# Samples' arrays of the second layer moved once per eight groups, and DeltaNet's diagonal blocks of 16 moved through scratch in 7 transfers a head

## The chip, the core and the metric

The kernel runs on one core of one Trainium2 chip, as one program of 54048 instructions. The metric is the device time of that core in microseconds (us). The engines are named as the profile names them: PE is the matrix engine (PEld its weight loads), DVE the vector engine, ACT the scalar engine, POOL the GpSimd engine, and SP the engine whose one queue issues every transfer of this kernel. SP issues them in the order in which they stand, and one that waits holds all that stand behind it.

## What is computed

One inference step of a two-layer recurrent model over a prompt of 2048 tokens and over 8 samples of one token each; all arithmetic is in 32-bit floats. Layer 0 runs an RG-LRU and a gated DeltaNet beside each other, layer 1 an S5 state space model:

```python
def trunk(x, c, ...):                      # once for the prompt, once for the samples
    for i in range(DEPTH):                 # DEPTH = 2
        h = rms_norm(x, w["norm_w"][i]) * (1.0 + scale) + shift
        if i % 2 == 0: y, ... = ab_mixer(h, ...)
        else:          y, sr, si = s5_mixer(h, ...)
        x = x + gate * y
    return rms_norm(x, w["final_norm_w"]), states

# gated DeltaNet, per head: chunks of 64 tokens
A = where(strict, einsum(k_beta, k) * decay, 0)
sol = triangular_solve(A + eye, rhs, lower=True)      # needs the inverse of A + I
S, o = scan over the chunks

# S5, per group of 16 channels (64 groups) and 64 complex states
Bu = einsum(B_bar, u);  Bu[0] += A_bar * x0
xs = associative_scan(A_bar, Bu)
y  = einsum(C, xs).real + d * u;  y = gelu(y);  ...
```

For the samples S5 is one step: state = A_bar * x0 + B_bar u, and the output is C state + d u.

## The kernel before

**Layer 0** runs in two halves of 1024 tokens (the first with the 8 samples beside it, so its arrays have 1032 columns), eight heads each. Each head is a row of products of the normed input with 128 columns of weights (the units k, xa, q, v, za, gw and zb). `in_unit` makes one of them: every product is three matmuls (high part by high part, high by low, low by high), PE's line L876, into groups of PSUM banks that ACT or DVE copies out. Halves with samples use groups of 384, 384 and 264 columns (`BLS`), the others two of 512 (`BL0`); four banks ("ps_mm") serve them.

**Background work.** Everything else is written as Python generators in a list (`Fibers`). `bg.pump` takes one step of each lane whenever 1536 columns of products have been written, so that DeltaNet, the RG-LRU, the S5 tables and S5 itself stand between the products in program order. A scheduler then orders each engine's instructions by its own estimate of times; instructions made through `VH` and `AH` (line L127) get a higher priority there. So a changed set of instructions can change the order of others, and engines wait for each other at run time wherever the estimate was off.

**DeltaNet's inverse** (`gdn_prep`, once per head, 16 times). It needs inverses of the 16x16 diagonal blocks of 8 chunks (64 blocks). A tile `AT` (128 partitions, 8 chunks, 128 columns) holds A transposed; its diagonal blocks go to DRAM scratch `fsd` in 8 transfers (L966) and come back as `fsA` with one block on each of 64 partitions (L970). Fifteen steps on DVE (`fsP` L1004, `fsT` L1006) make the inverses, `fsT`, and `fsU`, their transposes. Both are stored to scratch `fst` (L1010, L1011), and 16 small transfers read them back into three tiles: `zt` (even blocks), `zo` (odd blocks) and `U32` (block pairs of 32, zeroed by a GpSimd memset before, L1015). `gdn_main` of the same head uses them as weights on PE: `zt` at L1053, `zo` at L1065, `U32` after it.

**S5** (`s5`, lines L1702 to L1796) runs in two halves too, 8 blocks of 8 groups each; a block has two quads of 4 groups. Block i is added to lane i mod 2, so two blocks overlap. A quad loads three tables (`s5RT`, `s5ct`, `s5st`), PE projects (L1729), DVE rotates, scans and rotates back (`s5t`, ending with the sum X = X + ... that the text calls "the last sum"), a table `s5O` is loaded, and PE makes the output (L1786 with the table `MT`, L1787 with X and `s5O`).

In the first half a quad also carries the samples: it loads the old states `s5xa` and, with halves swapped, `s5xb` (one and two transfers), and their inputs `s5uo`. PE makes B u (L1740), ACT copies it, PE transposes it (L1749). DVE makes a·s5xa, b·s5xb, adds them, and adds what PE transposed; then PE multiplies by C (`cs8`, two transfers a block, L1776), DVE adds d·u, ACT applies gelu. New states and outputs (`dYs`) are stored for each quad. That makes 14 transfers a block for the samples. The second half (no samples) is the same code without them.

`s5_tables` (once per block, in the background of layer 0) loads a tile `gp` with five transfers, four of them for C.

Of the kernel before, what the change touches and what calls it, by code (L numbers as in the profile page):

```python
# [9 lines left out]
I32 = mybir.dt.int32  # L10
AF = mybir.ActivationFunctionType
OP = mybir.AluOpType
# [58 lines left out]
def hybrid_step(ctx: ExitStack, tc: tile.TileContext, I, O, dump=None):  # L71
# [14 lines left out]
    def K(name, shape, dt=FT):  # L86
        return kp.tile(list(shape), dt, name=name, tag=name)
# [23 lines left out]
    def D(name, shape, dt=FT):  # L111
        return dr.tile(list(shape), dt, name=name, tag=name)

    def dma(out, in_):
        SP.dma_start(out, in_)  # L115
# [33 lines left out]
    def bc(ap, shape):  # L149
        return ap.to_broadcast(list(shape))  # L150
# [30 lines left out]
    def wait(n):  # L181
        for _ in range(n):
            yield
# [291 lines left out]
    a1 = K("a1", (128, 2, 64))  # L475
# [151 lines left out]
    def s5_tables(mt):  # L627
# [5 lines left out]
        for off, x, y in ((624, "cre", "cim"), (752, "cim", "cre")):  # L633
            dma(gp[0:64, off:off + 128].rearrange("p (g c) -> p g c", c=16), I[x][:, g8])
            dma(gp[64:128, off:off + 128].rearrange("p (g c) -> p g c", c=16), I[y][:, g8])
# [96 lines left out]
    fsd = [D(f"fsd{i}", (8, 128, 16)) for i in range(2)]  # L732
    fst = [D(f"fst{i}", (2, 64, 256)) for i in range(2)]
    ss0 = {1: K("ss0", (128, 8))}
# [177 lines left out]
    def gdn_prep(hf, h, g, ready):  # L912
# [54 lines left out]
        for b in range(8):  # L967
            dma(fd[:, 16 * b:16 * b + 16, :].rearrange("u j i -> j u i"),
                AT[16 * b:16 * b + 16, :, 16 * b:16 * b + 16])
        F = TT("fsA", (64, 16, 16))  # L970
        dma(F.rearrange("p j i -> p (j i)"),
            fd.rearrange("u (b j) i -> (u b) (j i)", b=8))
# [40 lines left out]
        zt, zo = TT("zt", (128, 8, 16)), TT("zo", (128, 8, 16))  # L1013
        U32 = g["U32"] = TT("U32", (128, 8, 32))
        G.memset(U32, 0.0)  # L1015
        fb = [ft[n].rearrange("(u b) (i j) -> b i u j", b=8, i=16) for n in range(2)]
        for b in range(4):
            r = 32 * b
            dma(zt[r:r + 16], fb[0][2 * b])
            dma(zo[r:r + 16], fb[1][2 * b + 1])  # L1020
            dma(U32[r:r + 16, :, 0:16], fb[1][2 * b])
            dma(U32[r + 16:r + 32, :, 16:32], fb[1][2 * b + 1])
# [679 lines left out]
    def s5(hf, mt, uc, yg, upad):  # L1702
        Q3 = (128, 4, 128)
        yield from wait(9)
# [3 lines left out]
        if hf == 0:  # L1708
            cs8 = TT("cs8", (128, 8, 16))
            dma(cs8[0:64], I["cre"][:, mt * 8:mt * 8 + 8])  # L1710
            dma(cs8[64:128], I["cim"][:, mt * 8:mt * 8 + 8])
            VH.tensor_scalar(cs8, cs8, nsg[:, 0:1], None, op0=OP.mult)
        for qd in range(2):
# [5 lines left out]
            if hf == 0:  # L1719
                xa_, xb_ = TT("s5xa", (128, 4, 8)), TT("s5xb", (128, 4, 8))  # L1720
                dma(xa_, I["s5x"][:, g4, :])
                dma(xb_[0:64], I["s5x"][64:128, g4, :])
                dma(xb_[64:128], I["s5x"][0:64, g4, :])
                uo = TT("s5uo", (16, 4, 8))
                dma(uo, dUs[mt].rearrange("(c g) b -> c g b", g=8)[:, qd * 4:qd * 4 + 4, :])
# [10 lines left out]
            if hf == 0:  # L1736

                ps = PS("ch", (128, 128))
                for j in range(4):
                    PE.matmul(ps[32 * j:32 * j + 32], upad[:, qd * 32:qd * 32 + 32], tl["RT"][:, j, :],  # L1740
                              start=True, stop=True)
                us = TT("s5us", (128, 128))
                AH.activation(us, ps, AF.Copy)
                VH.tensor_tensor(xa_, xa_, bc(a1[:, 0, g4, None], (128, 4, 8)), op=OP.mult)
                VH.tensor_tensor(xb_, xb_, bc(a1is[:, g4, None], (128, 4, 8)), op=OP.mult)
                VH.tensor_tensor(xa_, xa_, xb_, op=OP.add)
                yield from wait(2)
                pws = PS("ch", (128, 4, 40))
                PE.transpose(pws.rearrange("p j c -> p (j c)")[:, 0:128], us, ident)  # L1749
                VH.tensor_tensor(xa_, xa_, pws[:, :, 0:8], op=OP.add)  # L1750
                dma(O["s_s5"][:, g4, :], xa_)
# [21 lines left out]
            if hf == 0:  # L1773
                pys = PS("ch", (128, 4, 8))
                for j in range(4):
                    PE.matmul(pys[0:16, j, :], cs8[:, qd * 4 + j, :], xa_[:, j, :],  # L1776
                              start=True, stop=True)
                VH.tensor_tensor(uo, uo, bc(d16[:, g4, None], (16, 4, 8)), op=OP.mult)
                VH.tensor_tensor(uo, uo, pys[0:16], op=OP.add)
                AH.activation(uo, uo, AF.Gelu_apprx_tanh)  # L1780
                dma(dYs[mt][:, qd * 32:qd * 32 + 32], uo.rearrange("c g b -> c (g b)"))
# [188 lines left out]
def layouts(x_prompt, x_sample, c_prompt, c_sample, state_conv_a, state_lru, state_conv_b,  # L1970
# [6 lines left out]
    def cols(v, n):  # L1977
# [30 lines left out]
        "s5x": np.concatenate([state_s5_re[0], state_s5_im[0]], axis=2).transpose(2, 1, 0),  # L2008
        "w1": c_in_w[0].reshape(8, 128, 16, 8, 16).transpose(2, 1, 0, 4, 3).reshape(16, 128, 1024),
# [8 lines left out]
        "cre": s5_c_re[0].transpose(2, 0, 1),  # L2018
        "cim": s5_c_im[0].transpose(2, 0, 1),
# [52 lines left out]
```

## Time and profile before

| | |
|---|---|
| median of 3 runs | 3163.17 us (3158.49 to 3163.83) |
| the profiled execution | 3162.53 us, its span 3160.6 us |
| busy: PE, DVE, ACT, POOL | 2946.8, 2077.0, 1109.6, 689.1 us |
| mean granted clock of PE | 0.967 of full speed |

The profile is of one execution. Its span runs from the first instruction to the last; some 2 us of the execution lie around it. Layer 0 takes most of it up to about 2130 us; S5's first half lies at about 2210 to 2525 us and its second at about 2700 to 2960 us, with products of layer 1 between and after. "Idle before" of an instruction is the time for which its engine had nothing to do right before it, and the name behind the arrow is what ended that.

### The profile page before, as it was taken

What the parts mean: (1) busy time and instruction counts of PE and PEld (TensorE: products, weight loads), DVE (VectorE), ACT (ScalarE), POOL (GpSimd) and SP (SyncE); (2) the same over time, 40 slices, a digit from 0 to 9 for tenths busy, and PEclk for the clock granted to TensorE, in tenths of its full rate; (3) what the DMA queues carried; (4) which work ended last, traced back from release to release, by engine and by line L of the source; (5) the groups of instructions that cost most, each with busy time, mean ns of one, the idle gap of its engine ahead of it and who ended that gap; (6) DMA issues with size and microseconds to landing.
All of it is one profiled execution on the core that took longest, in us unless ns stands there. A gap on an engine that the chain in (4) does not pass through costs nothing.

```text
span 3160.6 us, 54048 instructions
## 1 busy us (share of the span) xinstructions
PE 2946.8 (93%) x19958; PEld 2577.6 (82%) x19958; DVE 2077.0 (66%) x5468; ACT 1109.6 (35%) x2023; POOL 689.1 (22%) x672
## 2 busy tenths in 40 slices
PE   5999998999999999999999999999978899989998
PEld 3888888888887777777777777899868899877786
DVE  7896986677894877866756787445655534565524
ACT  3544444444543324433334343412211233110222
POOL 3233433223442323021111111101112222000100
PEclk8999999999999999999999999999989899999999
DMA  6344344443537873444434324555566548587442
GB/s 231 123 134 155 116 160 152 134 143 133 168 125 262 274 227 125 130 128 157 122 129 144 122 88 138 180 182 200 185 218 214 184 144 293 196 298 248 150 134 87
DMA packets 404136, 532.09 MB, mean 168 GB/s; under 512 B 143520, under 2 KB 210592, under 8 KB 403872
## 3 DMA queue, kind: packets, MB, share of 16 engines
q1 hardware_dynamic: 403872, 528.63, 51.0%
q8 instruction: 158, 2.59, 0.3%
q14 instruction: 106, 0.87, 0.1%
HBM read 328.11 MB, written 200.36 MB: 167 GB/s over the span
## 4 chain that ended last, share of the span: by engine, by line
PE 57%; DVE 26%; DMA 7%; issue 4%; ACT 2%; POOL 2%; SPq 2%; DVEq 0%; POOLq 0%; ACTq 0%
PE ps_mm L876 44%; DVE s5t L127 4%; DVE c_v L856 2%; SPq L115 2%; DVE xc L856 1%; DVE fsP L1004 1%; DMA yk<-yd 1%; DVE c_q L856 1%; DVE fsT L1006 1%; PE ps_pre L1787 1%; POOL wlo L234 1%; DVE D L910 1%; PE ps_ch L1139 1%; PE ps_ch L1145 1%; PE ps_pre L1786 1%
## 5 line engine op out<-in xcount | busy, mean ns | idle before, releaser
L876 PE MATMUL ps_mm<-hh,wlo 128*128 128x512 f32 (+2 forms) x2536 | 791.6, 373 | 0.0
L876 PE MATMUL ps_mm<-hh,whi 128*128 128x512 f32 (+2 forms) x2536 | 761.5, 361 | 4.7 <-DVE sz L1872 2.3
L876 PE MATMUL ps_mm<-hl,whi 128*128 128x512 f32 (+2 forms) x2536 | 748.7, 356 | 0.0
L876 PEld LDWEIGHTS ps_mm<-hl,whi 128*128 128x128 f32 x2536 | 480.2, 192 | 44.5 <-issue 0.2
L876 PEld LDWEIGHTS ps_mm<-hh,whi 128*128 128x128 f32 x2536 | 472.3, 192 | 53.5 <-DVE sz L1872 2.7
L876 PEld LDWEIGHTS ps_mm<-hh,wlo 128*128 128x128 f32 x2536 | 449.9, 192 | 35.7 <-issue 7.7
L234 POOL TENSOR_TENSOR wlo<-wraw,whi 128x512 fp32r<-128x512 f32 (+1 forms) x200 | 277.3, 1394 | 664.9 <-ACT whi L233 429.5
L876 PE MATMUL ps_mm<-yl,whi 128*128 128x512 f32 (+2 forms) x640 | 187.9, 356 | 3.0 <-DVE yl L234 3.0
L876 PE MATMUL ps_mm<-yh,whi 128*128 128x512 f32 (+2 forms) x640 | 185.1, 358 | 5.8 <-ACT yh L233 5.8
L876 PE MATMUL ps_mm<-yh,wlo 128*128 128x512 f32 (+2 forms) x640 | 189.8, 359 | 0.0
L233 ACT ACTIVATE whi<-wraw 128x512 fp32r<-128x512 f32 (+1 forms) x200 | 121.9, 618 | 119.5 <-DMA wraw<-in_wo 42.5
L1136 ACT ACTIVATE qs<-ps_ch,geg 128x128 f32<-128x128 f32 x128 | 47.1, 368 | 297.7 <-DVE rr L1133 293.8
L856 DVE SCALAR_TENSOR_TENSOR c_k<-raw,cbw,c_k 128x256 f32<-128x256 f32 x192 | 91.0, 513 | 73.7 <-ACT c_k L893 72.8
L876 PEld LDWEIGHTS ps_mm<-yh,whi 128*128 128x128 f32 x640 | 118.3, 191 | 17.9 <-ACT yh L233 7.3
L876 PEld LDWEIGHTS ps_mm<-yl,whi 128*128 128x128 f32 x640 | 119.9, 191 | 15.6 <-DVE yl L234 4.8
L876 PEld LDWEIGHTS ps_mm<-yh,wlo 128*128 128x128 f32 x640 | 118.3, 191 | 9.8
L892 ACT ACTIVATE raw<-ps_mm 128x384 f32<-128x384 f32 (+1 forms) x160 | 81.6, 513 | 74.4 <-PE ps_mm L876 70.9
L876 PE MATMUL ps_mm<-y2h,whi 128*128 128x384 f32 (+3 forms) x344 | 100.4, 340 | 0.1
L876 PE MATMUL ps_mm<-y2h,wlo 128*128 128x384 f32 (+3 forms) x344 | 99.9, 339 | 0.0
L876 PE MATMUL ps_mm<-y2l,whi 128*128 128x384 f32 (+3 forms) x344 | 99.6, 338 | 0.0
L856 DVE SCALAR_TENSOR_TENSOR c_v<-raw,cbw,c_v 128x256 f32<-128x256 f32 x192 | 95.1, 529 | 4.0 <-ACT c_v L893 3.8
L856 DVE SCALAR_TENSOR_TENSOR xc<-raw,caw,xc 128x256 f32<-128x256 f32 x192 | 94.7, 514 | 4.2 <-ACT xc L893 3.5
(669 smaller groups left out, 5754.2 us busy)
## 6 DMA issues: line engine op xcount, KB each, us to landing
wraw<-in_w SPq DMA_DIRECT2D x128, 256.0 KB, 3.8
whw<-whi SPq DMA_DIRECT2D x128, 256.0 KB, 2.5
wlw<-wlo SPq DMA_DIRECT2D x128, 256.0 KB, 2.4
whi<-whw SPq DMA_DIRECT2D x128, 256.0 KB, 4.4
wlo<-wlw SPq DMA_DIRECT2D x128, 256.0 KB, 4.2
modw<-in_modw SPq DMA_DIRECT2D x48, 512.0 KB, 5.7
yk<-yd SPq DMA_DIRECT2D x32, 512.0 KB, 5.8
xk<-x1d SPq DMA_DIRECT2D x32, 512.0 KB, 5.7
```

What stands on the lines that cost most here:

```text
L115: SP.dma_start(out, in_)
L127: return getattr(self.eng, op)(*args, **kw)
L233: a = A.activation(hi, src, AF.Identity)
L234: return a, (lo_eng or V).tensor_tensor(lo, src, f(hi), op=OP.subtract)
L856: V.scalar_tensor_tensor(d, raw[:, a * n + j:a * n + j + n], wt[:, tile_i, j:j + 1], d, op0=OP.mult, op1=OP.add)
L876: PE.matmul(p, w[:, c], x[:, b0:b1], start=(k == 0 and x is hh[k] and w is wh), stop=(k == 7 and w is wl))
L892: A.activation(raw[:, 3 + b0:3 + e], p[:, 0:e - b0], AF.Copy)
L910: V.tensor_scalar(dc[:, c], dc[:, c], tok["gc"][:, c, h:h + 1], 0.0, op0=OP.subtract, op1=OP.min)
L1004: V.tensor_tensor(pr_[:, 0:i, 0:i], Ti[:, 0:i, 0:i].rearrange("p j c -> p c j"), bc(F[:, 0:i, i].unsqueeze(1), s), op=OP.mult)
L1006: V.tensor_reduce(Ti[:, i, 0:i], pr_[:, 0:i, 0:i], axis=AX.X, op=OP.add, negate=True)
L1136: A.activation(qs, p1[:, 1, :], AF.Copy, scale=g["eg"][:, c:c + 1])
L1139: PE.matmul(p2_, U[:, c, :], rr, start=True, stop=True)
```

## The change

DeltaNet: `AT` is stored whole, in one transfer, to scratch whose rows are spaced so that the 16x16 blocks on the diagonal lie at one fixed stride, and `fsA` is read from there. `fst` is read back by three transfers over 128 (or 112) partitions: `zu` (all transposed blocks), `zt` and `zo`. The tile U32 is no longer zeroed and loaded; ACT makes its two halves from `zu` by a copy with a scale that is 0 or 1 on each partition (`odd`, made once at the start). S5: the inputs come in layouts that let `cs8`, `s5xa`, `s5xb`, `s5uo` be loaded by one transfer each per block; the three products with them on DVE are done once per block behind the load of `cs8`, and the new states and outputs are stored once per block. `s5_tables` takes two transfers for C where it took four.

```diff
         C8 = (128, 8, 16)
-        for off, x, y in ((624, "cre", "cim"), (752, "cim", "cre")):
-            dma(gp[0:64, off:off + 128].rearrange("p (g c) -> p g c", c=16), I[x][:, g8])
-            dma(gp[64:128, off:off + 128].rearrange("p (g c) -> p g c", c=16), I[y][:, g8])
+        for off, x in ((624, "cri"), (752, "cir")):
+            dma(gp[:, off:off + 128].rearrange("p (g c) -> p g c", c=16), I[x][:, g8])
         zero = TB("zero")
...
     gcd = [D(f"gcd{i}", (8, 8, 128)) for i in range(2)]
-    fsd = [D(f"fsd{i}", (8, 128, 16)) for i in range(2)]
+    fsd = [D(f"fsd{i}", (8, 128 * 129)) for i in range(2)]
     fst = [D(f"fst{i}", (2, 64, 256)) for i in range(2)]
...
+    oi, odd = TT("oddi", (128, 1), I32), K("odd", (128, 2))
+    G.iota(oi, pattern=[[0, 1]], base=0, channel_multiplier=1)
+    V.tensor_scalar(oi, oi, 4, 1, op0=OP.logical_shift_right, op1=OP.bitwise_and)
+    V.tensor_copy(odd[:, 1:2], oi)
+    V.tensor_scalar(odd[:, 0:1], odd[:, 1:2], -1.0, 1.0, op0=OP.mult, op1=OP.add)
     ss0 = {1: K("ss0", (128, 8))}
...
         fd, ft = fsd[par], fst[par]
-        for b in range(8):
-            dma(fd[:, 16 * b:16 * b + 16, :].rearrange("u j i -> j u i"),
-                AT[16 * b:16 * b + 16, :, 16 * b:16 * b + 16])
...
+        dma(fd[:, 0:128 * 128].rearrange("u (p i) -> p u i", i=128), AT)
         F = TT("fsA", (64, 16, 16))
-        dma(F.rearrange("p j i -> p (j i)"),
-            fd.rearrange("u (b j) i -> (u b) (j i)", b=8))
+        dma(F, fd.rearrange("u x -> (u x)").rearrange("(q x) -> q x", x=16 * 129)[:, 0:16 * 128]
+            .rearrange("q (j i) -> q j i", i=128)[:, :, 0:16])
         Ti = TT("fsT", (64, 16, 16))
...
         dma(ft[1], Tu.rearrange("p i j -> p (i j)"))
-        zt, zo = TT("zt", (128, 8, 16)), TT("zo", (128, 8, 16))
+        zt, zo, zu = (TT(n, (128, 8, 16)) for n in ("zt", "zo", "zu"))
         U32 = g["U32"] = TT("U32", (128, 8, 32))
-        G.memset(U32, 0.0)
-        fb = [ft[n].rearrange("(u b) (i j) -> b i u j", b=8, i=16) for n in range(2)]
-        for b in range(4):
-            r = 32 * b
-            dma(zt[r:r + 16], fb[0][2 * b])
-            dma(zo[r:r + 16], fb[1][2 * b + 1])
-            dma(U32[r:r + 16, :, 0:16], fb[1][2 * b])
-            dma(U32[r + 16:r + 32, :, 16:32], fb[1][2 * b + 1])
+        fb = [ft[n].rearrange("(u b) (i j) -> (b i) u j", b=8, i=16) for n in range(2)]
+        dma(zu, fb[1])
+        dma(zt, fb[0])
+        dma(zo[0:112], fb[1][16:128])
+        for t in range(2):
+            A.activation(U32[:, :, 16 * t:16 * t + 16], zu, AF.Copy, scale=odd[:, t:t + 1])
         while "v" not in ready:
...
         Q3 = (128, 4, 128)
+        g8 = slice(mt * 8, mt * 8 + 8)
+        if hf == 0:
+            G8 = (128, 8, 8)
+            xa_, xb_, uo = TT("s5xa", G8), TT("s5xb", G8), TT("s5uo", (16, 8, 8))
+            dma(xa_, I["s5x"][:, g8])
+            dma(xb_, I["s5xs"][:, g8])
+            dma(uo, dUs[mt].rearrange("(c g) b -> c g b", g=8))
         yield from wait(9)
...
             cs8 = TT("cs8", (128, 8, 16))
-            dma(cs8[0:64], I["cre"][:, mt * 8:mt * 8 + 8])
-            dma(cs8[64:128], I["cim"][:, mt * 8:mt * 8 + 8])
+            dma(cs8, I["cri"][:, g8])
             VH.tensor_scalar(cs8, cs8, nsg[:, 0:1], None, op0=OP.mult)
+            VH.tensor_tensor(xa_, xa_, bc(a1[:, 0, g8, None], G8), op=OP.mult)
+            VH.tensor_tensor(xb_, xb_, bc(a1is[:, g8, None], G8), op=OP.mult)
+            VH.tensor_tensor(xa_, xa_, xb_, op=OP.add)
+            VH.tensor_tensor(uo, uo, bc(d16[:, g8, None], (16, 8, 8)), op=OP.mult)
         for qd in range(2):
...
                 dma(tl[n].rearrange("p g n -> p (g n)"), src[mt][:, cs])
-            if hf == 0:
-                xa_, xb_ = TT("s5xa", (128, 4, 8)), TT("s5xb", (128, 4, 8))
-                dma(xa_, I["s5x"][:, g4, :])
-                dma(xb_[0:64], I["s5x"][64:128, g4, :])
-                dma(xb_[64:128], I["s5x"][0:64, g4, :])
-                uo = TT("s5uo", (16, 4, 8))
-                dma(uo, dUs[mt].rearrange("(c g) b -> c g b", g=8)[:, qd * 4:qd * 4 + 4, :])
+            l4 = slice(qd * 4, qd * 4 + 4)
             yield from wait(6)
...
                 AH.activation(us, ps, AF.Copy)
-                VH.tensor_tensor(xa_, xa_, bc(a1[:, 0, g4, None], (128, 4, 8)), op=OP.mult)
-                VH.tensor_tensor(xb_, xb_, bc(a1is[:, g4, None], (128, 4, 8)), op=OP.mult)
-                VH.tensor_tensor(xa_, xa_, xb_, op=OP.add)
                 yield from wait(2)
...
                 PE.transpose(pws.rearrange("p j c -> p (j c)")[:, 0:128], us, ident)
-                VH.tensor_tensor(xa_, xa_, pws[:, :, 0:8], op=OP.add)
-                dma(O["s_s5"][:, g4, :], xa_)
+                VH.tensor_tensor(xa_[:, l4], xa_[:, l4], pws[:, :, 0:8], op=OP.add)
+                if qd == 1:
+                    dma(O["s_s5"][:, g8, :], xa_)
             yield from wait(2)
...
                 for j in range(4):
-                    PE.matmul(pys[0:16, j, :], cs8[:, qd * 4 + j, :], xa_[:, j, :],
+                    PE.matmul(pys[0:16, j, :], cs8[:, qd * 4 + j, :], xa_[:, qd * 4 + j, :],
                               start=True, stop=True)
-                VH.tensor_tensor(uo, uo, bc(d16[:, g4, None], (16, 4, 8)), op=OP.mult)
-                VH.tensor_tensor(uo, uo, pys[0:16], op=OP.add)
-                AH.activation(uo, uo, AF.Gelu_apprx_tanh)
-                dma(dYs[mt][:, qd * 32:qd * 32 + 32], uo.rearrange("c g b -> c (g b)"))
+                VH.tensor_tensor(uo[:, l4], uo[:, l4], pys[0:16], op=OP.add)
+                if qd == 1:
+                    AH.activation(uo, uo, AF.Gelu_apprx_tanh)
+                    dma(dYs[mt], uo.rearrange("c g b -> c (g b)"))
             yield from wait(8)
...
         "s5x": np.concatenate([state_s5_re[0], state_s5_im[0]], axis=2).transpose(2, 1, 0),
+        "s5xs": np.concatenate([state_s5_im[0], state_s5_re[0]], axis=2).transpose(2, 1, 0),
         "w1": c_in_w[0].reshape(8, 128, 16, 8, 16).transpose(2, 1, 0, 4, 3).reshape(16, 128, 1024),
...
         "bim": s5_b_im[0].transpose(1, 0, 2),
-        "cre": s5_c_re[0].transpose(2, 0, 1),
-        "cim": s5_c_im[0].transpose(2, 0, 1),
+        "cri": np.concatenate([s5_c_re[0], s5_c_im[0]], axis=2).transpose(2, 0, 1),
+        "cir": np.concatenate([s5_c_im[0], s5_c_re[0]], axis=2).transpose(2, 0, 1),
         "s5d": s5_d[0].reshape(8, 8, 16),
```

Three places in the order of instructions are used below.

ACT, first head of the first half, after the RG-LRU's square root (`tt`) and ahead of the copies that free the PSUM groups of unit zb (`zbs`). Before:

```order
L1195 ACT_TABLE_LOAD
L1195 ACTIVATE tt_1402<-tt_1402 128x1032
L521 ACT_TABLE_LOAD
L521 ACTIVATE unit1_1648<-s5ab_1645 128x64
L1640 ACT_TABLE_LOAD
L1640 ACTIVATE zbs_1448<-ps_mm_1469 128x384
L1640 ACTIVATE zbs_1448<-ps_mm_1470 128x384
```

The same place with the change:

```order
L1197 ACT_TABLE_LOAD
L1197 ACTIVATE tt_1401<-tt_1401 128x1032
L1024 ACTIVATE U32_1555<-zu_1554,odd_174 128x8x16 x2
L1642 ACT_TABLE_LOAD
L1642 ACTIVATE zbs_1447<-ps_mm_1468 128x384
L1642 ACTIVATE zbs_1447<-ps_mm_1469 128x384
```

The two copies into U32 stand ahead of `zbs`, and they wait for the transfer that fills `zu`. In about 12 of the 16 heads they stand so, in the others near the copy of unit za.

SP, same head, from the stores of the inverses on. Before:

```order
L115 DMA fst_171<-fsT 64x256
L115 DMA fst_171<-fsU 64x256
L115 DMA whw_1_1_2027<-whi 128x512
L115 DMA wlw_1_1_2028<-wlo 128x512
L115 DMA zt<-fst_171 16x8x16
L115 DMA zo<-fst_171 16x8x16
L115 DMA U_1555<-fst_171 16x8x16 x2
L115 DMA zt<-fst_171 16x8x16
L115 DMA zo<-fst_171 16x8x16
```

With the change:

```order
L115 DMA fst_171<-fsT 64x256
L115 DMA fst_171<-fsU 64x256
L115 DMA whw_1_1_2015<-whi 128x512
L115 DMA wlw_1_1_2016<-wlo 128x512
L115 DMA zu<-fst_171 128x8x16
L115 DMA zt<-fst_171 128x8x16
L115 DMA zo<-fst_171 112x8x16
L115 DMA zd_165<-zbs 128x1024
L115 DMA yd<-gx 128x1024
```

Sixteen reads have become three, `zu` first; the weights' transfers around them kept their places.

PE, S5's first half, where the sample product of one quad (`s5xa` by `cs`) and the output of the quad before it (`MT`, then `s5O`) follow each other. Before, at the block whose C is cs8_26505:

```order
L876 MATMUL ps_mm<-hh,whi 128x384
L876 MATMUL ps_mm<-hl,whi 128x384
L876 MATMUL ps_mm<-hh,wlo 128x384
L1786 MATMUL ps_pre<-uc,MT 128x128 x2
L1776 MATMUL ps_ch<-s5xa,cs_26505 16x8 x4
L1787 MATMUL ps_pre<-s5t_26529,s5O_26635 128x128
L1786 MATMUL ps_pre<-uc,MT 128x128
```

The same block with the change (its C is cs8_26512); eleven rows of products of unit kind L881 (L876 before) follow the sample product, then the first one with `s5O`:

```order
L881 MATMUL ps_mm<-hh,whi 128x384 x2
L881 MATMUL ps_mm<-hl,whi 128x384 x2
L881 MATMUL ps_mm<-hh,wlo 128x384 x2
L1780 MATMUL ps_ch<-s5xa,cs_26512 16x8 x4
L1790 MATMUL ps_pre<-uc,MT 128x128
L881 MATMUL ps_mm<-hh,whi 128x264
L881 MATMUL ps_mm<-hl,whi 128x264
L881 MATMUL ps_mm<-hh,wlo 128x264
L881 MATMUL ps_mm<-hh,whi 128x264
```

From the third block on, the sample product of one quad stands directly ahead of the output of the quad before it at four places in the order before and at two with the change; at the others layer products stand between them.

DVE, S5's first half, around the addition of PE's transposed part to `s5xa` (row `s5xa<-s5xa,ps_ch`). Before, for the first quad of one block (its states are s5xa_26515), while the last sum of the quad ahead of it (s5t1_26529) is made:

```order
L127 TENSOR_TENSOR s5t1_26529<-s5st_26470,s5t2_26530 64x4x127 x2
L127 TENSOR_TENSOR s5xb_26516<-s5xb_26516,l1_25126 128x32
L127 SCALAR_TENSOR_TENSOR s5t2_26588<-rho8_145,l1_25126,s5t1_26587 128x128
L127 TENSOR_TENSOR s5t1_26529<-s5t1_26529,s5ct_26469 128x512
L127 TENSOR_TENSOR s5xa_26515<-s5xa_26515,s5xb_26516 128x32
L127 SCALAR_TENSOR_TENSOR s5t2_26588<-rho8_145,l1_25126,s5t1_26587 128x128
L127 TENSOR_TENSOR s5xa_26515<-s5xa_26515,ps_ch_26665 128x32
L127 SCALAR_TENSOR_TENSOR s5t2_26588<-rho8_145,l1_25126,s5t1_26587 128x128 x2
```

With the change, at the corresponding place (states s5xa_26441, quad ahead s5t1_26504):

```order
L127 TENSOR_TENSOR s5t1_26504<-s5st_26471,s5t2_26505 64x4x127 x2
L127 TENSOR_TENSOR s5t1_26595<-ps_pre_26590,s5ct_26520 128x512
L127 TENSOR_TENSOR s5t1_26504<-s5t1_26504,s5ct_26470 128x512
L127 TENSOR_TENSOR s5t2_26596<-ps_pre_26590,s5st_26521 64x512 x2
L127 TENSOR_TENSOR s5xa_26441<-s5xa_26441,ps_ch_26651 128x32
L127 TENSOR_TENSOR s5t1_26595<-s5t1_26595,s5t2_26596 128x512
L127 TENSOR_SCALAR l1_24828<-s5st_26521,nsg_83 128x4
L127 COPY l1_24828<-s5ct_26520 128x4
L127 SCALAR_TENSOR_TENSOR s5t2_26596<-rho8_145,l1_24828,s5t1_26595 128x128 x2
```

The addition stood behind the products with a and b and behind the quad's own first two scans; with the change those products are done far ahead, and the addition stands in front of the quad's own scans.

## Rows read from the trace of the kernel before

**Rows 1.** S5, both halves: length, busy us of each engine, granted clock, DMA share, GB/s.

```profile
2210.00:2525.00 315.00, 272.19 (x1885) 257.70 (x1885) 178.92 (x437) 64.84 (x144) 62.23 (x54) 0.92 0.64 202
...
2700.00:2960.00 260.00, 236.69 (x1196) 196.95 (x1195) 157.89 (x293) 33.60 (x58) 19.19 (x23) 0.97 0.71 240
```

**Rows 2.** Waits of PE, S5 first half: line, releaser: us, times, longest.

```profile
PE ps_ch L1776 <- DVE s5xa L127: 22.0, 6, 7.8
PE ps_pre L1787 <- DMA s5O<-dO: 5.8, 3, 2.2
```

**Rows 3.** Timeline of PE: start, length, instruction, idle before and releaser.

```profile
2328.65 0.38 PE L1776 MATMUL ps_ch<-s5xa,cs 128*16 128x8 f32 x8 [7.83 <-DVE s5xa L127]
2331.23 0.77 PE L1787 MATMUL ps_pre<-s5t,s5O 128*128 128x128 f32 x2 [2.20 <-DMA s5O<-dO]
...
2366.80 0.38 PE L1776 MATMUL ps_ch<-s5xa,cs 128*16 128x8 f32 x8 [3.27 <-DVE s5xa L127]
2368.84 0.77 PE L1787 MATMUL ps_pre<-s5t,s5O 128*128 128x128 f32 x2 [1.66 <-DMA s5O<-dO]
...
2478.23 0.36 PE L1776 MATMUL ps_ch<-s5xa,cs 128*16 128x8 f32 x8 [2.90 <-DVE s5xa L127]
2480.55 0.77 PE L1787 MATMUL ps_pre<-s5t,s5O 128*128 128x128 f32 x2 [1.97 <-DMA s5O<-dO]
```

**Rows 4.** Timeline of DVE before the wait at 2328.65.

```profile
2324.87 1.54 DVE L127 TENSOR_TENSOR_SCAN s5t<-rho,l,s5t 128x128 f32<-128x128 f32 x1
2326.34 1.68 DVE L127 TENSOR_TENSOR s5t<-s5t,s5ct 128x512 f32<-128x512 f32 x1
2327.94 0.18 DVE L127 TENSOR_TENSOR s5xa<-s5xa,s5xb 128x32 f32<-128x32 f32 x1
...
2328.44 0.15 DVE L127 TENSOR_TENSOR s5xa<-s5xa,ps_ch 128x32 f32<-128x32 f32 x1
```

**Rows 5.** Timeline of SP there.

```profile
2328.05 0.33 SPq L115 DMA_DIRECT2D s5O<-dO  x1
```

**Rows 6.** Waits of DVE, S5 first half.

```profile
DVE s5xb L127 <- DMA s5xb<-in_s5x: 13.1, 6, 4.3
```

**Rows 7.** Waits of PE, layer 0 (90 to 2080 us).

```profile
PE ps_pre L1053 <- DMA zt<-fst: 3.2, 2, 1.7
```

**Rows 8.** Timeline of SP, DeltaNet transfers of one head, one row of another.

```profile
332.79 3.63 SPq L115 DMA_DIRECT2D fsd<-AT  x8
337.58 0.46 SPq L115 DMA_DIRECT2D fsA<-fsd  x1
...
365.81 0.46 SPq L115 DMA_DIRECT2D fst<-fsU  x1
...
368.00 0.38 SPq L115 DMA_DIRECT2D zt<-fst  x1
...
376.07 0.91 SPq L115 DMA_DIRECT2D U<-fst  x2
...
1246.81 0.46 SPq L115 DMA_DIRECT2D fst<-fsU  x1
```

**Rows 9.** Transfers: count, KB each, median us from issue to landing.

```profile
dU<-ut SPq DMA_DIRECT2D x16, 512.0 KB, 3.5
...
fsA<-fsd SPq DMA_DIRECT2D x16, 64.0 KB, 2.7
...
fst<-fsU SPq DMA_DIRECT2D x16, 64.0 KB, 2.0
zt<-fst SPq DMA_DIRECT2D x64, 8.0 KB, 2.5
...
dMT<-k SPq DMA_DIRECT2D x8, 64.0 KB, 3.7
```

**Rows 10.** Timeline of ACT in the same two heads.

```profile
382.82 1.07 ACT L1195 ACTIVATE tt<-tt 128x1032 f32<-128x1032 f32 x1
...
1246.68 1.06 ACT L1195 ACTIVATE tt<-tt 128x1024 f32<-128x1024 f32 x1
```

## The prediction

> **What bounds the kernel.** I read the share of the engines first: PE is busy for 2946.8 of 3160.6 us in the table above, so only its idle time, 214 us in all, can be won by a change that leaves its matmuls alone, and this one does. Then the busy time by stage. S5's first half, the only stage that carries the samples, holds PE for 272.19 of 315 us, and its second half for 236.69 of 260 [rows 1]: 42.8 us idle against 23.3. The samples' arrays belong to the first half alone, so those 19.5 us more are what one would look at first. PE's waits in that stage name them: 22.0 us in six waits in front of the sample product (L1776), for DVE's last addition to `s5xa` [rows 2]. It is the largest wait there.
>
> The timeline of PE shows that this wait is not alone [rows 3]. At 2328.65 PE has stood 7.83 us for `s5xa`; right after the sample product it stands 2.20 us more for the table `s5O`. At 2366.80 it is 3.27 and then 1.66, at 2478.23 it is 2.90 and then 1.97. DVE's timeline ahead of the first of them shows why [rows 4]: the addition (2328.44) comes behind the quad's own scan (1.54 us), behind the last sum of the quad before (1.68) and the sum of the two products. And SP issues `s5O` at 2328.05 [rows 5], which is the end of that last sum (2326.34 + 1.68 = 2328.02): the load waits for a buffer that the sum frees. It lands 3.2 us later, when PE's wait ends. So the sample product and the output are both held by DVE, and whoever takes the first wait away meets the second.
>
> **The change in S5.** Eight blocks lose 8 of their 14 transfers, 64 in all. The loads of the old states move to the start of a block; DVE waited 13.1 us for `s5xb` in six waits [rows 6], which should go. DVE's own work falls a little: four small operations are done once a block in place of once a quad, 32 fewer in all; at 0.18 us each (the sum of the products in rows 4) that is some 6 us less on an engine that is busy 178.92 of 315 us [rows 1], off the path except where PE waits.
>
> What decides is the order. DVE's addition now stands ahead of the quad's own scans, and on PE two of the four places at which the sample product stood directly before the output have layer products in between. I give the four places their prices:
>
> - Two places get products in between; I take their waits to be those at 2366.80 and 2478.23, by position. 3.27 + 1.66 + 2.90 + 1.97 = 9.8 us of PE's idle time [rows 3], filled by products that stood behind them before. I count all of it.
> - At the other two, one of which is that at 2328.65, the output still follows at once and still waits for the last sum and for `s5O`. Only the last sum itself can come earlier: a scan of 1.54 us and the product with b stand no longer ahead of it, a shorter step of the rotation does. At the first of them the order also has some more layer products ahead. I take 2 us each, 4 us, between 0 and the 10.0 that was lost at 2328.65.
>
> S5 together: 9.8 + 4.0 = 13.8 us. Bounds: nothing, or a loss (below), at one end; at the other all of 22.0 + 5.8 [rows 2], 27.8 us.
>
> **The change in DeltaNet.** A head issues 27 transfers before and 7 after, 320 fewer over 16 heads.
>
> - A whole AT (512 KB in pieces of 512 bytes) replaces 8 transfers of diagonal blocks. Before: 8 issues of 3.63 us together, and from the first issue to that of `fsA` 337.58 - 332.79 = 4.8 us; `fsA` takes 2.7 [rows 8, 9]: 7.5 us. After: one of 512 KB, as `dU<-ut` is, 3.5 us; about 0.5 to the next issue; and `fsA` in 1024 pieces of 64 bytes, as `dMT<-k` of 64 KB has them, 3.7: 7.7 us. No change, between -1.5 (if `fsA` keeps 2.7 and the store is quicker) and +2 us a head; DVE's fifteen steps behind it have a whole head's products for cover, and the cost without cover would be 16 x 2 = 32 us at most.
> - The reads of `fst`: 16 issues from 368.00 to 376.98, 9.0 us, of which the last ones land some 2.5 us later [rows 8, 9]. After: three issues of about 0.5 us, landing within 3.7. The last of them is there some 6 us sooner. PE waited for `zt` only 3.2 us, in two waits [rows 7]. These were in a head in which the first reads were late, not the last, and `zt` is now second behind `zu` and 1.2 us slower. I count 1 us won, between 0 and 3.2.
> - U32 by ACT. Two small copies a head, each far fewer elements than the root of 1.07 us ahead of them [rows 10], on an ACT that is busy 35% of the span. They wait for `zu`, and in ACT's order `zbs` stands behind them, whose copies free PSUM banks for PE. `zu` lands about 2.0 + 0.4 + 3.7 = 6.1 us after `fsU`'s store is issued [rows 8, 9]. In one head that store goes out at 365.81, so `zu` is there at 371.9, and ACT reaches the place at 382.82 + 1.07 = 383.9 [rows 8, 10]: 12 us to spare. In the head with the least to spare the store goes out at 1246.81 and ACT is there at 1247.7: it would stand until 1252.9, 5.2 us. PE then has two more banks to write into, so I count nothing; without that cover it is 5.2 us, once. GpSimd's memset goes, which nobody waited for.
> - 400 fewer issues take some 180 us off SP's queue, by 3.63 / 8 = 0.45 us for one of those in rows 8. In layer 0 PE does not wait for weights in any row that I found, so I count nothing for it, between 0 and 5.
>
> By the Trainium skill, page "DMA: Bandwidth & Descriptors", section on the anatomy of one DMA, each transfer has a fixed part of about 2.0 us whatever its size; 400 fewer would be an estimated 800 us if they ran one after the other. The trace says they do not: sixteen go out in 9.0 us though each takes about 2 to land. The same page, in its specifications, wants pieces of at least 512 bytes, and the four reads of 64-byte pieces go against it. The trace agrees as to the direction, 3.7 against 2.7 us for 64 KB; by that rule the sum would lose about 1 us a read, which the cover above takes.
>
> **The sum.** 13.8 + 1 = 14.8 us off the profiled execution, 3162.53 - 14.8 = 3147.7 us. That execution lies 0.6 us under the median of the runs, 3163.17, so I leave the figure as it is. On this kernel 0.2%, 6.3 us, is about what a measurement can tell from no change.
>
> **Rivals.**
>
> - *The wait only changes its name.* PE no longer stands before the sample product but stands longer before the output, for the last sum and `s5O`, since SP may issue `s5O` only when the sum is done. For it: rows 3 and 5, where the second wait ends just so. Against: two of four places now have products in between. Gain 0 to 3 us with DeltaNet's: about 3160 us.
> - *Everything goes.* With shorter queues on SP and DVE the loads come early and both waits vanish: 27.8 + 3.2 = 31 us, 3131.5 us. For it: the second half of S5 with the same scans idles 19.5 us less, and DVE is idle for 40% of the stage. Against: that half has waits of its own, so its level alone gives 3143.
> - *Slower: DVE stands at the addition.* It now stands in front of the quad's scans and needs what PE transposes (L1749). Should PE come to the transpose 3 us after DVE has done the rotation, each of 16 quads holds its scans by 3 us, 48 in all; with half on the path through the last sum and `s5O`, +24 against -14.8: 3172 us. For it: PE makes layer products between projection and transpose. Against: DVE's rotation and the other quad's last sum (1.68 us) take up most of that time. It decides from about 2 us of lateness a quad, where 16 us on the path cancel the gain.
> - *That it doesn't do what it says* has no room: the transfers are gone from SP's order.
>
> **Chances.** Forecast 0.50, from 3138 to 3156 us; everything goes 0.14; name only 0.20; slower 0.16. Faster by over 0.2% therefore 0.64, within 0.2% 0.20, slower 0.16. The range 3130 to 3170 leaves out the far half of the slower case and a little of the fast one.
>
> **What would show it.** In S5's first half PE's wait for `s5xa` falls from 22.0 to under 8 us, that for `s5O` and `s5t` in front of the output does not grow by as much, and PE's idle time there falls from 42.8 to about 29. DVE's waits for `s5xb` are gone; a wait of DVE for PE's transpose of over 20 us would speak for the slower case. In layer 0, ACT's waits for `zu` add up to under 10 us, PE's waits for `zt` stay under 3 us, and `fsA` lands in 3 to 4 us. The forecast is wrong if the gain is made in layer 0, or if the wait at the output takes up what the sample product gave.

## The result, and the profile after

The change takes 3124.44 us (median of 4 runs, 3120.99 to 3131.38) against 3163.5 us before: a ratio of 0.988, interval 0.9856 to 0.9904. Run a second time it took 3130.23 us, ratio 0.9904 (0.9882 to 0.9926). So 31 to 39 us are gone where 14.8 were forecast; the first time lies below the range that was given, the second at its lower end.

To see where, both traces are cut at the same transfers: the store of `zbs` of each head and the transfer `dU<-ut` of each block. Three stretches of the kernel before, from the second to the third such store of layer 0 and the two parts of S5's first half (columns as in rows 1):

```profile
272.02:395.68 123.66, 114.20 (x1003) 106.97 (x1002) 97.18 (x284) 55.43 (x114) 48.71 (x51) 0.94 0.41 131
2225.04:2454.62 229.58, 195.41 (x1385) 184.03 (x1384) 129.21 (x307) 42.90 (x99) 46.39 (x42) 0.93 0.68 214
2454.62:2715.56 260.94, 250.90 (x1584) 245.09 (x1583) 119.57 (x210) 78.18 (x137) 54.76 (x40) 0.97 0.58 200
```

The same three of the kernel after:

```profile
270.67:386.15 115.48, 108.96 (x1004) 102.22 (x1003) 98.54 (x284) 54.53 (x114) 48.61 (x49) 1.00 0.44 140
2205.84:2426.02 220.18, 193.38 (x1385) 182.76 (x1384) 124.45 (x282) 41.93 (x92) 48.47 (x42) 0.94 0.72 228
2426.02:2676.62 250.60, 246.88 (x1584) 241.66 (x1583) 116.78 (x202) 77.64 (x136) 57.36 (x40) 0.99 0.60 204
```

The stretch in layer 0 is 8.2 us shorter: 2.9 of them idle time of PE (9.5 to 6.5), the rest busy time of the same matmuls, at a granted clock of 1.00 in place of 0.94. S5's first half is 19.7 us shorter in its two parts together: 13.7 of idle time (44.2 to 30.5) and 6.0 of busy time. The other stretches of layer 0 together give 11.0 us, none more than 3.2. Over the whole span (3160.6 to 3119.0) PE's busy time fell from 2946.8 to 2931.8 us with the same number of matmuls.

One trace of each kernel is little for S5. In the trace of the second measurement (`e10_again`) its two parts are 13.2 us shorter than before, 10.8 of them idle time, and layer 0 is 18.9 us shorter in all. Over the seven traces here without the change in S5 the two parts take 490.9 us on the mean, over the ten with it 477.0. So S5 gives about 14 us, and 19.7 is a favourable pair of traces.

PE's largest waits in S5's first half after the change, to be set beside rows 2:

```profile
PE ps_pre L1791 <- DMA s5O<-dO: 11.0, 2, 7.0
PE ps_mm L881 <- DVE sz L1876: 7.4, 4, 3.8
PE ps_ch L1780 <- DVE s5xa L127: 5.9, 4, 2.2
PE ps_pre L1791 <- DVE s5t L127: 3.3, 1, 3.3
```

The wait for `s5xa` fell from 22.0 to 5.9 us, and part of it came back as forecast: the wait for `s5O` rose from 5.8 to 11.0, and the one for `sz` of the layer products from 2.3 to 7.4.

The prediction priced four places. Counted in order of time they are the 7th, 9th, 13th and 15th of the 16 sample products. The 9th and the 15th (2366.80 and 2478.23 in rows 3) have no wait left, before the sample product or before the output, which gives the 9.8 us that were counted. The other two stayed tight. The 7th is the one at 2328.65 in rows 3; the 13th before:

```profile
2441.08 0.38 PE L1776 MATMUL ps_ch<-s5xa,cs 128*16 128x8 f32 x8 [6.73 <-DVE s5xa L127]
2442.34 0.77 PE L1787 MATMUL ps_pre<-s5t,s5O 128*128 128x128 f32 x2 [0.88 <-POOL s5t L1768]
```

The 7th and the 13th after, where the second wait is now the longer one:

```profile
2298.81 0.38 PE L1780 MATMUL ps_ch<-s5xa,cs 128*16 128x8 f32 x8 [1.91 <-DVE s5xa L127]
2306.14 0.77 PE L1791 MATMUL ps_pre<-s5t,s5O 128*128 128x128 f32 x2 [6.96 <-DMA s5O<-dO]
...
2410.28 0.36 PE L1780 MATMUL ps_ch<-s5xa,cs 128*16 128x8 f32 x8 [1.36 <-DVE s5xa L127]
...
2415.08 0.76 PE L1791 MATMUL ps_pre<-s5t,s5O 128*128 128x128 f32 x2 [4.02 <-DMA s5O<-dO]
```

The two waits together fell from 10.0 to 8.9 us at the 7th and from 7.6 to 5.4 at the 13th: 1.2 and 2.2 us, where 2 each were forecast. All four places give 13.2 us (13.5 in `e10_again`).

DVE's waits there (rows 6 before): `s5xb` is gone, and what PE transposes is waited for 0.2 us in place of 4.0; but `s5uo`, whose product now stands early, is waited for 40.6 us (12.1 before).

```profile
DVE s5uo L127 <- DMA s5uo<-dUs: 40.6, 6, 11.8
```

The DeltaNet transfers after (rows 9): one whole A takes 3.5 us, the reads in 64-byte pieces 3.1 and 3.9.

```profile
fsd<-AT SPq DMA_DIRECT2D x16, 512.0 KB, 3.5
...
fsA<-fsd SPq DMA_DIRECT2D x16, 64.0 KB, 3.1
...
zu<-fst SPq DMA_DIRECT2D x16, 64.0 KB, 3.9
zt<-fst SPq DMA_DIRECT2D x16, 64.0 KB, 3.9
```

ACT's idle time in front of its copies into U32, over all heads:

```profile
  DMA zu<-fst: 3.5, 2
```

### The profile page after: what moved, and what is told of

The parts are those of the page before. It is cut to its first block, busy times and chain, and to the rows that moved or that the text cites. A ratio compares the mean times of both kernels' runs of the same rounds, so it can differ in the third digit from the quotient of the medians.

```text
span 3119.0 us, 53357 instructions
## 1 busy us (share of the span) xinstructions
PE 2931.8 (94%) x19958; PEld 2567.0 (82%) x19958; DVE 2067.1 (66%) x5439; ACT 1115.1 (36%) x2046; POOL 687.6 (22%) x657
## 5 line engine op out<-in xcount | busy, mean ns | idle before, releaser
L881 PE MATMUL ps_mm<-hh,wlo 128*128 128x512 f32 (+2 forms) x2536 | 786.9, 372 | 0.0
L881 PE MATMUL ps_mm<-hh,whi 128*128 128x512 f32 (+2 forms) x2536 | 755.9, 360 | 8.7 <-DVE sz L1876 7.7
L881 PE MATMUL ps_mm<-hl,whi 128*128 128x512 f32 (+2 forms) x2536 | 742.8, 354 | 0.0
L881 PEld LDWEIGHTS ps_mm<-hh,whi 128*128 128x128 f32 x2536 | 469.6, 191 | 58.1 <-DVE sz L1876 8.9
L881 PEld LDWEIGHTS ps_mm<-hl,whi 128*128 128x128 f32 x2536 | 477.7, 191 | 44.7 <-issue 0.4
L881 PEld LDWEIGHTS ps_mm<-hh,wlo 128*128 128x128 f32 x2536 | 446.8, 192 | 36.0 <-issue 7.9
L881 PE MATMUL ps_mm<-yh,whi 128*128 128x512 f32 (+2 forms) x640 | 186.4, 360 | 7.6 <-ACT yh L233 6.9
L881 PE MATMUL ps_mm<-yh,wlo 128*128 128x512 f32 (+2 forms) x640 | 190.2, 360 | 0.0
L881 PE MATMUL ps_mm<-yl,whi 128*128 128x512 f32 (+2 forms) x640 | 187.1, 356 | 0.5 <-DVE yl L234 0.4
L233 ACT ACTIVATE whi<-wraw 128x512 fp32r<-128x512 f32 (+1 forms) x200 | 121.7, 617 | 115.5 <-DMA wraw<-in_w 37.9
L881 PEld LDWEIGHTS ps_mm<-yh,whi 128*128 128x128 f32 x640 | 118.6, 192 | 20.1 <-ACT yh L233 8.2
L881 PEld LDWEIGHTS ps_mm<-yl,whi 128*128 128x128 f32 x640 | 120.6, 192 | 12.5 <-DVE yl L234 1.0
L881 PEld LDWEIGHTS ps_mm<-yh,wlo 128*128 128x128 f32 x640 | 118.1, 191 | 9.7
L881 PE MATMUL ps_mm<-y2h,whi 128*128 128x384 f32 (+3 forms) x344 | 100.0, 340 | 0.0
L881 PE MATMUL ps_mm<-y2h,wlo 128*128 128x384 f32 (+3 forms) x344 | 99.8, 339 | 0.0
L881 PE MATMUL ps_mm<-y2l,whi 128*128 128x384 f32 (+3 forms) x344 | 99.6, 338 | 0.0
L861 DVE SCALAR_TENSOR_TENSOR c_q<-raw,cbw,c_q 128x256 f32<-128x256 f32 x192 | 94.4, 527 | 5.2 <-ACT c_q L898 5.0
```

The costliest lines, as they stand in the source:

```text
L233: a = A.activation(hi, src, AF.Identity)
L861: V.scalar_tensor_tensor(d, raw[:, a * n + j:a * n + j + n], wt[:, tile_i, j:j + 1], d, op0=OP.mult, op1=OP.add)
L881: PE.matmul(p, w[:, c], x[:, b0:b1], start=(k == 0 and x is hh[k] and w is wh), stop=(k == 7 and w is wl))
```

## The experiments

Each was timed beside the kernel before on one chip; the medians of that kernel were 3159 to 3162 us. The traces are of one execution each.

**The parts, one by one.** Each kernel is before with some hunks of the diff.

```diff
 e1_s5:     + hunks of s5 (loads, products and stores once per block)
 e2_gdn:    + hunks of gdn_prep, fsd and odd
 e3_store:  + of these: fsd, one store of AT, read of fsA
 e4_reads:  + of these: zu, zt, zo, U32 by ACT
 e5_tables: + hunk of s5_tables only
 e6_nogp:   the whole change without the hunk of s5_tables
```

> S5's sample arrays once per block, alone; layer 0 as before. If the 19.7 us that S5's first half gave come from this part, this kernel is at about 3144 us (3163.5 - 20) and its layer 0 ends where that of before does, within 3 us. If part of S5's gain needs the changed layer 0 (transfers that run ahead of S5, another order), it stands at 3150 to 3158.

Measured 3148.83 us, 0.9951 (0.9929 to 0.9973). PE's waits in S5's first half are those of the whole change:

```profile
PE ps_pre L1789 <- DMA s5O<-dO: 11.0, 2, 6.6
...
PE ps_ch L1778 <- DVE s5xa L127: 5.4, 4, 2.2
```

So the S5 part is what moved these waits, and it needs no changed layer 0. Its gain of 13.1 us lies between the two that were expected, and near the 13.8 of the prediction's term for S5.

> DeltaNet's 7 transfers a head alone; S5 and its tables as before. If the 19 us won in layer 0 are DeltaNet's, about 3144 us, with S5's first half as long as before. If they come from the two loads fewer in the tables of S5, which run beside the second head where 8 us were won, about 3152 to 3160 us.

3149.2 us, 0.9955 (0.9939 to 0.9971).

> Only the store of A transposed in one transfer and the read of the blocks from it (9 transfers to 2), reads of the inverses as before. By the count of issues on SP's queue (112 of the 320 fewer) about a third of DeltaNet's gain, 6 us: 3157. If the gain is that of the reads alone, 3163. If the diagonal blocks come sooner to DVE's fifteen steps and that is the gain, about 3146.

3150.09 us, 0.9959 (0.9941 to 0.9976).

> Only the reads of the inverses (16 transfers to 3) with U32 made by ACT. By the count of issues (208 of 320) two thirds of DeltaNet's gain, 13 us: 3151. If the queue has nothing to do with it, 3160 to 3164; if PE's or ACT's wait for zu costs time, above 3164.

3147.35 us, 0.9951 (0.9934 to 0.9968).

Neither count of issues fits: a third of the transfers, two thirds, and both together each win the same 12 to 15 us.

> Only the tables of S5 with two loads in place of four, 16 transfers fewer in all. If the parts add up, 39 us less S5's 13 and DeltaNet's 13 leave 13 for this part: about 3150 us. If the parts reinforce each other and this one is next to nothing, 3158 to 3164.

3149.74 us, 0.9961 (0.9942 to 0.9981): 16 transfers fewer of some 2340 win 12 us.

> The whole change without the two loads fewer in the tables of S5. If the parts add up and the tables hold the rest, 3163 - 13 - 13 = about 3137 us; if the tables are nothing and S5 and DeltaNet gain more together, 3124 to 3128.

3134.01 us, 0.9913 (0.989 to 0.9937), and beside it later the change itself:

> The change itself once more, beside the others on one chip. If the tables' loads add to S5 and DeltaNet as measured, 3124 us, some 10 below the kernel without them (3134).

3130.23 us, 0.9904. The tables that won 12 us alone add about 4 to the rest, within the intervals. Three edits that share no line win the same, once. What their traces have in common is one place: the stretch of layer 0 that took 123.7 us takes 114.9 in `e3_store` and `e4_reads` and 114.4 in `e5_tables`.

**The place.** It lies around 285 us of the kernel before (timelines: start, length, instruction, idle time before it and releaser).

SP's timeline, before:

```profile
263.12 0.91 SPq L115 DMA_DIRECT2D U<-fst  x2
...
264.60 0.38 SPq L115 DMA_DIRECT2D gp<-dG  x1
...
266.84 0.59 SPq L115 DMA_DIRECT2D gp<-in_cre  x1
...
277.18 0.32 SPq L115 DMA_DIRECT2D yd<-gx  x1
277.55 1.25 SPq L115 DMA_DIRECT2D wraw<-in_w  x2
```

ACT's timeline, before:

```profile
281.74 0.63 ACT L233 ACTIVATE whi<-wraw 128x512 fp32r<-128x512 f32 x1 [2.77 <-DMA wraw<-in_w]
```

POOL's timeline, before:

```profile
274.74 2.41 POOL L1208 TENSOR_TENSOR gx<-sz,tt 128x1024 f32<-128x1024 f32 x1 [2.46 <-DVE slru L1206]
...
278.32 2.10 POOL L1074 COPY U<-U 32x256 f32<-32x256 f32 x4
282.50 1.26 POOL L234 TENSOR_TENSOR wlo<-wraw,whi 128x512 fp32r<-128x512 f32 x1 [2.08 <-ACT whi L233]
283.72 1.10 POOL L651 TENSOR_TENSOR Rt<-gp 128x512 f32<-128x512 f32 x1
```

PE's timeline, before:

```profile
285.70 0.63 PE L669 MATMUL ps_pre<-ident,R 128*128 128x128 f32 x4 [3.00 <-DVE raw L888]
...
291.42 0.42 PE L876 MATMUL ps_mm<-hl,whi 128*128 128x264 f32 x1
291.64 0.42 PE L876 MATMUL ps_mm<-hh,wlo 128*128 128x264 f32 x1
```

Busy time of the engines and granted clock of 20 us (columns as in rows 1), before:

```profile
280.00:300.00 20.00, 17.00 (x132) 15.39 (x130) 5.60 (x17) 7.02 (x16) 2.77 (x4) 0.70 0.33 114
```

The loads of `gp` follow the reads of U32 at 264.60 to 267.4. POOL's product `Rt` from them runs at 283.72 only, though they land within 3.7 us: in POOL's order it stands behind four copies of U, done at 280.42, and behind `wlo`, which then waited 2.08 us more for ACT. ACT in turn had stood 2.77 us for `wraw`, the weights that it splits. SP issued that load at 277.55, directly behind the store `yd<-gx`, which had to wait for POOL's `gx` (274.74 + 2.41 = 277.15). So what ended the wait is not `gp` but a load of weights that stood behind a store on SP's queue. The chain that the profile follows back (its critical view) names it too, between SP's issue and `whi`:

```profile
277.55 4.17 DMA wraw<-in_w
```

DVE's sum of R needs `Rt`, PE's transpose needs that, and PE stands 3.00 us (put down to `raw`, DVE's instruction after that sum). Then two products of 264 columns start 0.22 us apart, 1.2 columns a ns: PE runs at the lower of its two clocks, 1.2 GHz, and the granted clock of the 20 us is 0.70. The kernel after, at the same table of S5:

SP's timeline, after:

```profile
254.84 0.79 SPq L115 DMA_DIRECT2D zo<-fst  x1
...
256.28 0.91 SPq L115 DMA_DIRECT2D wraw<-in_w  x2
257.28 0.38 SPq L115 DMA_DIRECT2D gp<-dG  x1
...
258.18 0.43 SPq L115 DMA_DIRECT2D gp<-in_cir  x1
```

POOL's timeline, after:

```profile
270.23 1.10 POOL L650 TENSOR_TENSOR Rt<-gp 128x512 f32<-128x512 f32 x1
```

The same 20 us, after:

```profile
280.00:300.00 20.00, 20.00 (x193) 17.77 (x192) 13.37 (x49) 9.94 (x22) 5.99 (x8) 1.00 0.47 158
```

The loads go out 7 us earlier, `wraw` (256.28) ahead of them, and `Rt` has moved on POOL, ahead of the RG-LRU's products and of the copies of U. PE has no idle time there and the clock stays 1.00. The orders of POOL, before:

```
L1208 TENSOR_TENSOR gx_2967<-sz_2711,tt_2969 128x128x8
L234 TENSOR_TENSOR wlo_3216<-wraw_3026,whi_3215 128x512
L1074 COPY U_3229<-U32_3094 32x8x32 x4
L234 TENSOR_TENSOR wlo_3220<-wraw_3211,whi_3219 128x512
L651 TENSOR_TENSOR Rt_3286<-gp_3149 128x512
```

and after:

```
L234 TENSOR_TENSOR wlo_3184<-wraw_3007,whi_3183 128x512
L234 TENSOR_TENSOR wlo_3188<-wraw_3179,whi_3187 128x512
L650 TENSOR_TENSOR Rt_3254<-gp_3119 128x512
L1202 TENSOR_TENSOR gx_2948<-gx_2948,tt_2950 128x1032
...
L1076 COPY U_3197<-U32_3076 32x8x32 x4
```

`Rt` stands behind the copies of U in before, `e1_s5` and the control below, and in their traces ACT stands 2.8 us for `wraw` ahead of it and PE has the wait of 3.0 us. It stands ahead of them in `e2_gdn`, `e3_store`, `e4_reads`, `e5_tables`, `e6_nogp` and after, where SP issues the weights that ACT needs there earlier; theirs have neither wait. Another order by the scheduler is thus what the three parts share; why it comes with fewer transfers is not shown. What the place costs is not a fixed 8.2 us: with the same wait the stretch takes 120.4 us in `e1_s5` and 121.7 in the control, against 114.4 to 115.5 in the six without. That is 5 to 9 us, less than the 12 that each part wins; the rest of the 12 is not located.

**A control**: same transfers, another order of the sixteen reads.

```diff
+for b in range(4): dma(zt[...])   # then all zo, then U32
```

> A control: the kernel before with its sixteen reads of the inverses in another order (all into zt, then zo, then U32), the same count and bytes. If fewer transfers are what won time in layer 0, this stays at 3160 to 3164 us. If any other sequence of instructions is rid of a stretch of low clock that the kernel before happens to have beside the second head, it is at 3150 like the single parts.

3159.27 us, 0.999 (0.9974 to 1.0006), PE's wait 3.02 us at 283.56. Another sequence alone is not enough.

**Transfers put back.**

```diff
+for j in range(20): dma(dumd[par][j], 8 KB of fst)   # e15_dum4: range(4)
```

> The whole change with 20 transfers of 8 KB a head put back, from scratch to scratch, which nothing waits for, right behind the three reads. If SP's issues and the load on the queue are what layer 0 paid for, its 12 to 19 us come back: 3137 to 3144 us. If the count of transfers as such is not the cause, 3124 to 3128.

3162.03 us, 1.0001 (0.9985 to 1.0017): the whole gain is gone, though S5's first half stays short (482.1 against 490.5 us before). The same place:

SP's timeline in `e8_dummy`:

```profile
258.52 10.48 SPq L115 DMA_DIRECT2D dumd<-fst  x16
...
279.02 1.80 SPq L115 DMA_DIRECT2D dumd<-fst  x3
280.91 0.53 SPq L115 DMA_DIRECT2D gp<-dG  x1
...
286.11 1.03 SPq L115 DMA_DIRECT2D wraw<-in_w  x2
```

ACT's timeline in it:

```profile
290.79 0.63 ACT L233 ACTIVATE whi<-wraw 128x512 fp32r<-128x512 f32 x1 [4.63 <-DMA wraw<-in_w]
```

PE's timeline in it:

```profile
294.69 1.09 PE L668 MATMUL ps_pre<-ident,R 128*128 128x128 f32 x4 [5.39 <-DVE R L663]
```

Busy time and clock of two stretches in it:

```profile
280.00:300.00 20.00, 14.61 (x175) 12.93 (x174) 9.23 (x19) 5.39 (x14) 5.20 (x7) 0.82 0.65 223
300.00:320.00 20.00, 20.00 (x101) 17.67 (x99) 3.08 (x18) 5.37 (x13) 3.61 (x3) 0.50 0.27 90
```

Now `gp` goes out at 280.91, behind the needless transfers, and `wraw` at 286.11. It is again `wraw` that comes last: ACT stands 4.63 us for it. PE's wait is 5.39 us, and the 20 us after it run at a granted clock of 0.50, wholly at 1.2 GHz. But the place is a small part of what the 320 transfers cost: beside the trace of `e10_again` layer 0 is 31.2 us longer, 6.3 of them in this stretch and 15.8 in the one that spans its two halves, for a reason that is open.

> The change with 4 needless transfers of 8 KB a head, 64 in all. If each transfer on the queue costs layer 0 its share (20 a head cost some 32 to 38 us), 6 to 8 us above the change, 3136 to 3138. If only single places pay, where a load comes too late for the one who needs it, then 4 a head, 2 us of the queue, cost nothing: 3128 to 3132.

3132.57 us, 0.9904 (0.9877 to 0.9931), the ratio of the change. Sixty-four transfers cost nothing that can be measured; but the intervals are as wide as the 6 to 8 us that a price for each would make, so it does not settle the question. The traces do not settle it either: layer 0 ends at 2208.8 us here, and at 2205.8, 2206.1 and 2213.7 in after, `e10_again` and `e11_oearly`, whose layer 0 is the change's own. That the price is paid only where a load, or an order made for it, comes too late fits the place, and is not shown beyond it.

**The place removed without fewer transfers.**

```diff
 # s5_tables, e9_later on before, e12_later on after
-yield from wait(2)
+yield from wait(4)
```

> The kernel before with one number changed: the tables of S5 wait four steps of the background in place of two between their loads and DVE's first use of them. No transfer fewer. If 8 us or more of layer 0's gain come from DVE no longer standing for these loads (PE's wait of 3 us in front of the transpose of R, and the stretch of low clock after it), this is at about 3150 us like the two loads fewer. If the count of transfers is needed, 3158 to 3164.

3157.68 us, 0.9986 (0.9972 to 0.9999). PE's wait is gone, although ACT stands 3.5 us for `wraw` here too: the stretch of layer 0 took 110.4 us at clock 1.00 (123.7 before), and the next 8.8 less. So the wait and the low clock can go without a transfer fewer. But the time is not the 3150 us expected for that: the tables now reach into later heads, some of whose stretches lengthened by up to 10 us (102.4 to 112.7, 104.7 to 112.0, 107.1 to 111.8) while another shortened (120.8 to 107.7). The total therefore does not tell what the place alone is worth.

> The change with the four steps in the tables. DVE's remaining waits for these loads (6.7 us of cs for gp) go; PE hardly waited for them any more, so 3120 to 3125 us; slower, above 3126, if the longer preparation of tables comes into the way of layer 1.

3148.89 us, 0.996 (0.9943 to 0.9977), slower than the change, with the same longer heads.

**The rest of S5's wait.**

```diff
 # e11_oearly, e14_uo_o: o1 = TB("s5O1"); dma(o1, dO...) moved up to the loads of RT, ct, st
 # e13_uo, e14_uo_o: uo * d16 moved down to the first addition of pys
```

> The change with the table s5O of a quad loaded with its other three tables, not behind its scans. If PE's remaining wait at the output (11.0 us for s5O in S5's first half, 2 waits) is only the late load, it is gone and the kernel is at 3110 to 3116 us. If the load just waits for another buffer, no change, 3124.

3128.58 us beside 3130.23 of the change: no difference. PE's waits in S5's first half:

```profile
PE ps_pre L1791 <- DVE s5t L127: 19.4, 6, 4.4
PE ps_ch L1780 <- DVE s5xa L127: 4.5, 3, 2.3
```

The wait for `s5O` is gone and that for DVE's last sum has grown from 3.3 to 19.4: the output is held by the sum, and the wait for the load had hidden it.

> The change with the product of the samples' inputs with d (uo) put back to where its result is used. With the change DVE stood 40.6 us for that load in S5's first half, in six waits. If these stand on the path to the last sum and the output, 4 to 10 us below the change, 3120 to 3126; if DVE's scans wait for their tables anyway, the same time, 3128 to 3132.

3131.59 us, 0.9898 (0.9867 to 0.9929). It does not tell: in its trace DVE still stands for the load, 44.8 us, since the scheduler put the product early again.

```profile
DVE s5uo L127 <- DMA s5uo<-dUs: 44.8, 6, 11.9
```

> The same with the table s5O loaded early as well. Alone that took PE's 11.0 us wait for s5O away and gave nothing, since the output then waited for the last sum. If the last sum is late because DVE stands for uo, both together win 10 us or more on the change, about 3118; otherwise 3126 to 3132.

3126.66 us, 0.9884 (0.9859 to 0.9909); DVE's wait for `s5uo` 26.0 us, PE's for the last sum 19.9. Within the intervals this is the change again; no version beat it clearly.

## Why the prediction was wrong

- *S5's waits*: right in kind, place by place: 13.8 us were forecast for the four places, 13.2 were found (13.5 in `e10_again`). The wait for `s5xa` fell below 8 us, the wait at the output grew by less, DVE did not stand at the addition, and the rival of a changed name and the one of everything gone both failed. That the idle time of the two parts fell by 13.7 us is partly luck, as other waits of PE moved too; in `e10_again` it fell by 10.8.
- *"only its idle time ... can be won"*: this step failed. The sum priced each wait at its own idle time. With the same matmuls PE's busy time fell by 15.0 us of 41.6 in the first trace and by 16.2 of 32.9 in `e10_again`. In the first trace 6.0 of that lie in S5's first half and 5.2 in the stretch of layer 0, where the granted clock is 0.94 with the stop of PE and 1.00 without it. The row that showed it was there: 0.92 in the first half against 0.97 in the second (rows 1).
- *DeltaNet, transfer by transfer*: right. `fsA` landed in 3.1 us (forecast 3.7), `zu` in 3.9 (3.7), one A in 3.5 (3.5), ACT stood 3.5 us for `zu` in all, and PE no longer waits for `zt`. By the Trainium skill, page "DMA: Bandwidth & Descriptors", section "Specifications", pieces under 512 bytes do not reach line rate; the trace agrees, 3.1 against 2.7 us for `fsA`. DVE waited 2.8 us in all for `fsA`, 5.8 before.
- *"400 fewer issues ... I count nothing for it, between 0 and 5"*: this step failed. Layer 0 gave 19.2 us in the first trace and 18.9 in the second, which is what the prediction itself had named as a sign of being wrong. It had looked for rows in which PE waits for weights. What waited was POOL's part of S5's tables, and PE through DVE (3.0 us, put down to `raw`). At the end of that chain there was a load of weights after all, `wraw`, which SP issued late behind a store; but PE's row named neither a load nor SP. Some 5 to 9 us are shown to be there. The other 10 or more lie spread over the heads. That the number of transfers matters is shown by `e8_dummy`, in which layer 0 is longer than before (2237.3 against 2225.0 us); through which places is open.

## What to carry to other kernels

A transfer taken out changes where the scheduler puts the work that needs the transfers behind it, on every engine; look for instructions that stand late in another engine's order, and follow a wait back to its end: here one put down to DVE ended, through POOL and ACT, at a load behind a store on SP's queue. Price a wait of TensorE at its idle time plus the stretch of lower clock behind it, which the windows show. When several small edits each win the same, test them together before adding them up. Read the size of a gain from more than one trace.

## What was not expected of the hardware

After a stop of 3.0 us PE ran at 1.2 GHz for part of the next stretch (granted clock 0.70 over 20 us; 0.83 over the same 20 us in `e1_s5` and `e7_order`, with about the same stop), after one of 5.39 us for all of the following 20 us (0.50). Of needless transfers of 8 KB, sixty-four cost nothing that could be measured to within some 8 us, and 320 cost 32 us.
